# Butterflies and spectrum products of a long convolution moved from GpSimd to VectorE

## The chip, the cores and the metric

The kernel runs on one core of one Trainium2 chip. The metric is the device time of one execution in microseconds; several executions are taken, and their median counts. The core has TensorE (matmul, in the profile PE, its weight loads PEld), VectorE (DVE), ScalarE (ACT), GpSimd (POOL) and SyncE (SP, which issues the DMA transfers). Each engine takes its own instructions in order; semaphores hold an instruction until what it reads or overwrites is ready.

## What is computed

The reference is one layer of a hybrid backbone on 1024 latent tokens and 256 context tokens: a SwiGLU block, a mixer with four head groups, a second SwiGLU block, all in float32. The change lies in group B of the mixer, a Hyena long convolution of order 2 on 256 channels:

```
def long_conv(u, kf, bias):
    L = u.shape[1]
    U = jnp.fft.rfft(u, n=2 * L, axis=1)
    y = jnp.fft.irfft(U * kf[None], n=2 * L, axis=1)[:, :L]
    return y + u * bias

y = x1 * long_conv(v, kf[:, 0], bias[0])
y = x2 * long_conv(y, kf[:, 1], bias[1])
```

It is done once for the latents (L = 1024) and once for the context (L = 256). The other groups are windowed attention, dense attention and a gated linear attention (GLA).

## The kernel before

The kernel goes through the first SwiGLU block, the filters' spectra, the second half of that block, the projections with the mixer, the output projection and the second SwiGLU block. Matmuls of the big products are done three times per tile (L984 to L986): each operand is split into a high part, made on ScalarE (L56), and a low part, made on VectorE or GpSimd (L62).

A convolution splits time into 128 rows of J (8 for the latents, 2 for the context). The forward transform multiplies each of the J slices with a cosine and a sine matrix on TensorE (`forward_dft`, L217) and joins the J results by butterflies (`fft`, L120 to L168). Then comes the complex product with the filter's spectrum K (L365 to L370), a second `fft` into Z, which is the buffer of K, and the inverse matmuls (L380, L381), whose results are added to `u` times the bias and multiplied by the gate (L383, L385). For the latents this is done for two groups of 128 channels (`g`) and two orders (`o`), four passes one after another: each pass needs the result of the one before, or at least its buffers. For the context there are two passes of 256 channels, and J = 2 leaves `fft` after two operations of its first stage.

In `fft` the first stage gives sums `a` and differences `b`. The sums lead by `c` and `d` (L148, L149) to the rows with even number (L150 to L153), and this half ran on GpSimd; the differences lead to the odd rows (L158 to L166) on VectorE. Each operation is a separate instruction over all 128 partitions. The inverse matmuls take the rows in the order 0, 7, 6, 5, so they begin with an even one and go on with an odd one.

Around the convolution stand the projections (L984 to L986, evacuated by ScalarE at L1404, L1485 and L1491), the preparation of attention's queries and keys (`attn_prep`, L613 to L635: on ScalarE, VectorE and GpSimd), and, at higher priority, the context's convolution and its attention (L688 maxima, L702 their transposition, L762 and L763 scores, L740 values, L786 sums). A planner sets the order: it simulates the program's timeline with costs of its own and puts into each engine's queue what it thinks can run next. So an edit of one operation's engine changes the order of much around it, on all engines, until the output projection. `hyena_spectra` calls `fft` too, with buffers of its own, in the first SwiGLU block.

Of the kernel before, what the change touches and what calls it, by code (L numbers as in the profile page):

```python
# [12 lines left out]
ALU = mybir.AluOpType  # L13
# [102 lines left out]
def swp(a):  # L116
    return a[:, ::-1]


def fft(E, pool, J, W, stage1, dst, halves=None):  # L120

    nc = E.nc
    if J == 2:
        stage1(0, 1, ALU.add, dst[:, :, 0:1])
        stage1(0, 1, ALU.subtract, dst[:, :, 1:2])
        return
    if halves is None:  # L130
        a = pool.tile([128, 2, 4, W], F32, tag="fa", name="fa")
        b = pool.tile([128, 2, 4, W], F32, tag="fb", name="fb")
        for lo in (0, 2):
            stage1(lo, 2, ALU.add, a[:, :, lo:lo + 2])
        for lo in (0, 2):
            stage1(lo, 2, ALU.subtract, b[:, :, lo:lo + 2])
    else:
        a, b = halves

    def pair(f_re, f_im):  # L140
        step = f_im - f_re + J
        flat = dst.rearrange("p r j w -> p (r j) w")
        return flat[:, f_re:f_re + step + 1:step]

    g = nc.gpsimd
    c = pool.tile([128, 2, 2, W], F32, tag="fc", name="fc")
    d = pool.tile([128, 2, 2, W], F32, tag="fd", name="fd")
    g.tensor_tensor(out=c, in0=a[:, :, 0:2], in1=a[:, :, 2:4], op=ALU.add)  # L148
    g.tensor_tensor(out=d, in0=a[:, :, 0:2], in1=a[:, :, 2:4], op=ALU.subtract)  # L149
    g.tensor_tensor(out=pair(0, 0), in0=c[:, :, 0], in1=c[:, :, 1], op=ALU.add)  # L150
    g.tensor_tensor(out=pair(4, 4), in0=c[:, :, 0], in1=c[:, :, 1], op=ALU.subtract)
    g.tensor_tensor(out=pair(2, 6), in0=d[:, :, 0], in1=swp(d[:, :, 1]), op=ALU.add)
    g.tensor_tensor(out=pair(6, 2), in0=d[:, :, 0], in1=swp(d[:, :, 1]), op=ALU.subtract)  # L153

    v = nc.vector
    A, P = (pool.tile([128, 2, W], F32, tag=f"f{n}", name=f"f{n}") for n in "AP")
    B, M, e, f = (b[:, :, n] for n in (0, 1, 2, 3))
    v.tensor_tensor(out=A, in0=b[:, :, 0], in1=swp(b[:, :, 2]), op=ALU.add)  # L158
    v.tensor_tensor(out=B, in0=b[:, :, 0], in1=swp(b[:, :, 2]), op=ALU.subtract)
    v.tensor_tensor(out=P, in0=b[:, :, 1], in1=b[:, :, 3], op=ALU.add)  # L160
    v.tensor_tensor(out=M, in0=b[:, :, 1], in1=b[:, :, 3], op=ALU.subtract)
    v.tensor_tensor(out=e, in0=M, in1=swp(P), op=ALU.add)
    v.tensor_tensor(out=f, in0=swp(P), in1=M, op=ALU.subtract)
    for o, s, src, base in ((pair(1, 7), R_HALF, e, A), (pair(5, 3), -R_HALF, e, A),
                            (pair(3, 5), R_HALF, f, B), (pair(7, 1), -R_HALF, f, B)):
        v.scalar_tensor_tensor(out=o, in0=src, scalar=s, in1=base, op0=ALU.mult, op1=ALU.add)  # L166


def fft_from_dft(E, pool, J, W, banks, dst):

    nc = E.nc
    if J == 2:
        keep = pool.tile([128, 2, W], F32, tag="fk", name="fk")
        nc.scalar.activation(out=keep, in_=banks[1], func=ACTF.Copy)

        def stage1(lo, n, op, out):
            nc.vector.tensor_tensor(out=out.rearrange("p r j w -> p (r j) w"), in0=banks[0], in1=keep, op=op)
    else:
        keep = {}
        for q in (2, 3):  # L180
            k = pool.tile([128, 2, 2, W], F32, tag=("fc", "fd")[q - 2], name="fk")
            nc.scalar.activation(out=k, in_=banks[q], func=ACTF.Copy)
            keep[q] = k

        def stage1(lo, n, op, out):
            q = lo // 2
            nc.vector.tensor_tensor(out=out.rearrange("p r j w -> p j r w"), in0=banks[q], in1=keep[q + 2], op=op)
    fft(E, pool, J, W, stage1, dst)


def fft_from_sbuf(E, pool, J, W, src, dst):
    nc = E.nc

    def stage1(lo, n, op, out):
        h = J // 2
        nc.vector.tensor_tensor(out=out, in0=src[:, :, lo:lo + n], in1=src[:, :, lo + h:lo + h + n], op=op)
    fft(E, pool, J, W, stage1, dst)


def alloc_banks(E, J, W):  # L200
# [114 lines left out]
def hyena(E, P, seq, zrows, cw, cb, bias, dft, kspec, mixg, y_out):  # L315

    nc = E.nc
    J = 8 if seq == "lat" else 2
    T = 128 * J
    W = 128 if seq == "lat" else 256  # L320
    G = 256 // W
    pool = P["hy"]
# [31 lines left out]
    for g in range(G):  # L354
        u = token_major(0, g, "u")
        for o in range(2):
            X = pool.tile([128, 2, J, W], F32, tag="X", name="X")
            K = pool.tile([128, 2, J, W], F32, tag="K", name="K")
            E.load(K, kspec[o, g])
            forward_dft(E, pool, J, W, load_mats, u, X)  # L360
            b3 = bias[:, o, g * W:(g + 1) * W]
            nc.gpsimd.tensor_tensor(out=u, in0=u, in1=b3.unsqueeze(1).to_broadcast([128, J, W]), op=ALU.mult)
            t1 = pool.tile([128, J, W], F32, tag="fa", name="t1")
            t2 = pool.tile([128, J, W], F32, tag="fb", name="t2")
            nc.gpsimd.tensor_tensor(out=t1, in0=X[:, 0], in1=K[:, 0], op=ALU.mult)  # L365
            nc.vector.tensor_tensor(out=t2, in0=X[:, 0], in1=K[:, 1], op=ALU.mult)
            nc.vector.tensor_tensor(out=X[:, 0], in0=X[:, 1], in1=K[:, 1], op=ALU.mult)
            nc.vector.tensor_tensor(out=X[:, 1], in0=X[:, 1], in1=K[:, 0], op=ALU.mult)
            nc.gpsimd.tensor_tensor(out=X[:, 0], in0=t1, in1=X[:, 0], op=ALU.subtract)
            nc.vector.tensor_tensor(out=X[:, 1], in0=t2, in1=X[:, 1], op=ALU.add)  # L370
            gate = token_major(1 + o, g, "gate")
            Z = K
            fft_from_sbuf(E, pool, J, W, X, Z)
            jb = 512 // W
            for j0 in range(0, J, jb):
                ps = E.psum("s").rearrange("p (j w) -> p j w", j=jb)
                for j in range(jb):
                    f = (J - (j0 + j)) % J
                    m = load_mats(1, j0 + j)
                    nc.tensor.matmul(ps[:, j], lhsT=m[:, 0], rhs=Z[:, 0, f], start=True, stop=False)  # L380
                    nc.tensor.matmul(ps[:, j], lhsT=m[:, 1], rhs=Z[:, 1, f], start=False, stop=True)  # L381
                js = slice(j0, j0 + jb)
                nc.vector.tensor_tensor(out=u[:, js], in0=ps, in1=u[:, js], op=ALU.add)  # L383
                dst = u[:, js] if o == 0 else ytm[:, js, g * W:(g + 1) * W]
                nc.vector.tensor_tensor(out=dst, in0=u[:, js], in1=gate[:, js], op=ALU.mult)  # L385
            yield
# [1409 lines left out]
```

## Time and profile before

| | us |
|---|---|
| median of 3 runs | 2956.24 |
| the runs | 2952.4, 2956.24, 2982.59 |
| the profiled execution | 2959.08 |
| its span (first to last instruction) | 2957.3 |

| engine | busy us | share of the span |
|---|---|---|
| TensorE, matmul | 2749.6 | 93% |
| TensorE, weight load | 2180.1 | 74% |
| VectorE | 1898.0 | 64% |
| ScalarE | 1133.4 | 38% |
| GpSimd | 1118.4 | 38% |

The busy share is a mean over stages with different limits. A matmul's recorded length holds some overlap with its neighbour, so starts are the better measure of its pace. A group view gives for each kind of instruction how often and how long it ran and what ended the idle time in front of it; the order of time gives single instructions; the windows view gives a stretch's busy times with the granted TensorE clock, where 1.00 is 2.4 GHz and 0.50 is 1.2 GHz.

### The profile page before, as it was taken

How to read it: one execution, taken by the hardware profiler on the slowest of the kernel's cores; microseconds unless marked ns; L12 is line 12 of the kernel's file. 1: busy time of each engine (PE TensorE's matmuls, PEld its weight loads, DVE VectorE, ACT ScalarE, POOL GpSimd, SP SyncE). 2: the span in 40 equal slices, each digit the busy share in tenths (PEclk: the TensorE clock that was granted, in tenths of full speed). 3: DMA queues.
4: the chain of work that ended last, by engine and by line, in shares of the span. 5: the costliest groups of instructions: out<-in, count | busy, mean ns of one | idle time of the engine just before them, and what ended most of it. 6: DMA issues, size and time to landing. Idle time of an engine off the chain costs nothing.

```text
span 2957.3 us, 39868 instructions
## 1 busy us (share of the span) xinstructions
PE 2749.6 (93%) x14088; PEld 2180.1 (74%) x14088; DVE 1898.0 (64%) x3135; ACT 1133.4 (38%) x2051; POOL 1118.4 (38%) x980
## 2 busy tenths in 40 slices
PE   7899988899999888888988989989899999999998
PEld 5886776678788787776754544477898888878888
DVE  4978677754899955767657666662956555533447
ACT  5742222223333642224424434553743333333444
POOL 1334355544000214546415425463435555520002
PEclk9999999999999999899978979999999999999999
DMA  8654755342877563342462110264652222244445
GB/s 296 214 179 139 210 111 125 79 150 93 281 250 263 175 209 113 121 138 84 140 167 50 37 40 12 85 234 157 216 173 97 85 77 84 86 175 149 145 138 202
DMA packets 278460, 427.02 MB, mean 144 GB/s; under 512 B 97417, under 2 KB 163954, under 8 KB 276852
## 3 DMA queue, kind: packets, MB, share of 16 engines
q1 hardware_dynamic: 278260, 424.47, 44.6%
q8 instruction: 111, 1.82, 0.3%
q14 instruction: 89, 0.73, 0.1%
HBM read 345.14 MB, written 79.13 MB: 143 GB/s over the span
## 4 chain that ended last, share of the span: by engine, by line
PE 43%; DVE 5%; DMA 2%; issue 1%; ACT 1%; POOL 1%; SPq 0%; DVEq 0%; POOLq 0%; ACTq 0%
PE ps L986 11%; PE ps L984 10%; PE ps L985 10%; PE ps L740 2%; PE ps L762 1%; PE ps L688 1%; PE ps L763 1%; PE ps L550 1%; PE ps L535 1%; DVE wl L62 1%; DMA gd<-zf 1%; DVE mx L692 1%; PE ps L786 0%; PE ps L546 0%; PE ps L1139 0%
## 5 line engine op out<-in xcount | busy, mean ns | idle before, releaser
L56 ACT ACTIVATE wh<-raw 128x512 fp32r<-128x512 f32 x661 | 408.7, 625 | 513.6 <-PE ps L986 225.0
L62 POOL TENSOR_TENSOR wl<-raw,wh 128x512 fp32r<-128x512 f32 x221 | 328.1, 1489 | 558.1 <-ACT wh L56 342.1
L62 DVE TENSOR_TENSOR wl<-raw,wh 128x512 fp32r<-128x512 f32 x440 | 331.7, 760 | 170.9 <-ACT wh L56 113.2
L985 PE MATMUL ps<-gs,wh 128*128 128x512 f32 (+1 forms) x1056 | 376.5, 357 | 7.0 <-DVE gs L62 7.0
L986 PE MATMUL ps<-gs,wl 128*128 128x512 f32 (+1 forms) x1056 | 373.8, 356 | 2.9 <-DVE wl L62 2.9
L984 PE MATMUL ps<-gs,wh 128*128 128x512 f32 (+1 forms) x1056 | 351.8, 358 | 9.6 <-ACT gs L56 5.0
L984 PE MATMUL ps<-xh,wh 128*128 128x256 f32 (+2 forms) x952 | 320.8, 337 | 12.2 <-ACT zev L1404 5.6
L986 PE MATMUL ps<-xh,wl 128*128 128x256 f32 (+2 forms) x952 | 319.6, 337 | 10.9 <-POOL wl L62 6.4
L985 PE MATMUL ps<-xl,wh 128*128 128x256 f32 (+2 forms) x952 | 323.3, 340 | 0.0
L984 PE MATMUL ps<-t,wh 128*128 128x512 f32 x704 | 281.0, 399 | 11.0 <-DVE up L1077 6.2
L986 PE MATMUL ps<-t,wl 128*128 128x512 f32 x704 | 280.2, 399 | 1.9 <-DVE wl L62 1.9
L985 PE MATMUL ps<-t,wh 128*128 128x512 f32 x704 | 280.5, 398 | 0.0
L984 PE MATMUL ps<-b,wh 128*128 128x512 f32 x528 | 212.6, 403 | 20.6 <-DVE up L1074 19.7
L984 PEld LDWEIGHTS ps<-gs,wh 128*128 128x128 f32 x1056 | 200.3, 190 | 40.7 <-ACT gs L56 5.4
L985 PEld LDWEIGHTS ps<-gs,wh 128*128 128x128 f32 x1056 | 200.9, 190 | 35.9 <-DVE gs L62 7.7
L986 PEld LDWEIGHTS ps<-gs,wl 128*128 128x128 f32 x1056 | 200.5, 190 | 32.4 <-DVE wl L62 3.7
L56 ACT ACTIVATE wh<-s 128x512 fp32r<-128x512 f32 x176 | 110.4, 630 | 295.3 <-PE ps L985 152.1
L985 PE MATMUL ps<-b,wh 128*128 128x512 f32 x528 | 211.5, 401 | 0.0
L986 PE MATMUL ps<-b,wl 128*128 128x512 f32 x528 | 210.9, 399 | 0.2 <-POOL wl L62 0.2
L984 PEld LDWEIGHTS ps<-xh,wh 128*128 128x128 f32 (+1 forms) x952 | 182.3, 192 | 37.5 <-ACT zev L1404 7.2
L986 PEld LDWEIGHTS ps<-xh,wl 128*128 128x128 f32 (+1 forms) x952 | 181.8, 191 | 37.2 <-POOL wl L62 9.1
L919 POOL TENSOR_TENSOR tmp<-tmp 128x512 f32<-128x512 f32 (+1 forms) x18 | 24.7, 1374 | 482.1 <-ACT tmp L917 482.1
(369 smaller groups left out, 5906.5 us busy)
## 6 DMA issues: line engine op xcount, KB each, us to landing
raw<-in_w SPq DMA_DIRECT2D x308, 512.0 KB, 3.5
stg<-in_wmT SPq DMA_DIRECT2D x56, 512.0 KB, 4.1
hid<-g SPq DMA_DIRECT2D x88, 256.0 KB, 2.0
g<-hid SPq DMA_DIRECT2D x88, 256.0 KB, 2.7
m<-in_dft_lat SPq DMA_DIRECT2D x128, 128.0 KB, 2.7
raw<-in_wo SPq DMA_DIRECT2D x24, 512.0 KB, 3.8
x<-in_xT SPq DMA_DIRECT2D x36, 256.0 KB, 4.5
stg<-in_wmp SPq DMA_DIRECT2D x16, 512.0 KB, 10.6
```

What stands on the lines that cost most here:

```text
L56: nc.scalar.activation(out=hi, in_=src, func=ACTF.Copy)
L62: low = eng.tensor_tensor(out=lo, in0=src, in1=hi.bitcast(F32), op=ALU.subtract)
L535: nc.tensor.matmul(ps[:, t], lhsT=kt[32 * h:32 * h + 32, ts], rhs=qt[32 * h:32 * h + 32, ts], start=True, stop=True, tile_position=(32 * h ...
L550: nc.tensor.matmul(ps[:, i0:i0 + 64], lhsT=S[64 * p:64 * p + 64, c], rhs=qt[64 * p:64 * p + 64, 64 * c:64 * c + 64], start=False, stop=c % ...
L688: nc.tensor.matmul(ps, lhsT=qs, rhs=k1[:, lo:hi], start=True, stop=mo is None)
L692: nc.vector.tensor_reduce(out=mx[:, hh * nqt + t, bi:bi + 1], in_=ps, axis=AX.X, op=ALU.max)
L740: mm = nc.tensor.matmul(O[64 * hh:64 * hh + 64, s], lhsT=V[:, kt], rhs=p[hh], start=j == 0, stop=j == last)
L762: nc.tensor.matmul(ps, lhsT=k1[:, ks], rhs=q1[:, hh, a:b], start=True, stop=False)
L763: nc.tensor.matmul(ps, lhsT=k2[:, ks], rhs=q2[:, hh, a:b], start=False, stop=not banded)
L984: nc.tensor.matmul(ps, lhsT=wh(k), rhs=xh(k), start=start and k == 0, stop=False, skip_group_check=loose)
L985: nc.tensor.matmul(ps, lhsT=wh(k), rhs=xl(k), start=False, stop=False, skip_group_check=loose)
L986: nc.tensor.matmul(ps, lhsT=wl(k), rhs=xh(k), start=False, stop=stop and k == nk - 1, skip_group_check=loose)
```

## The change

`fft` gets a parameter `g`, the engine of the even half. The two callers in the convolution, `fft_from_dft` and `fft_from_sbuf`, pass VectorE; `hyena_spectra` passes nothing and stays on GpSimd. In the product, the first of the four multiplications (L365) and the subtraction (L369) go to VectorE as well.

```
-def fft(E, pool, J, W, stage1, dst, halves=None):
+def fft(E, pool, J, W, stage1, dst, halves=None, g=None):
...
-    g = nc.gpsimd
+    g = g or nc.gpsimd
     c = pool.tile([128, 2, 2, W], F32, tag="fc", name="fc")
     d = pool.tile([128, 2, 2, W], F32, tag="fd", name="fd")
     g.tensor_tensor(out=c, in0=a[:, :, 0:2], in1=a[:, :, 2:4], op=ALU.add)
...
-    fft(E, pool, J, W, stage1, dst)
+    fft(E, pool, J, W, stage1, dst, g=nc.vector)
...
-            nc.gpsimd.tensor_tensor(out=t1, in0=X[:, 0], in1=K[:, 0], op=ALU.mult)
+            nc.vector.tensor_tensor(out=t1, in0=X[:, 0], in1=K[:, 0], op=ALU.mult)
             nc.vector.tensor_tensor(out=t2, in0=X[:, 0], in1=K[:, 1], op=ALU.mult)
             nc.vector.tensor_tensor(out=X[:, 0], in0=X[:, 1], in1=K[:, 1], op=ALU.mult)
             nc.vector.tensor_tensor(out=X[:, 1], in0=X[:, 1], in1=K[:, 0], op=ALU.mult)
-            nc.gpsimd.tensor_tensor(out=X[:, 0], in0=t1, in1=X[:, 0], op=ALU.subtract)
+            nc.vector.tensor_tensor(out=X[:, 0], in0=t1, in1=X[:, 0], op=ALU.subtract)
```

On VectorE, in the second `fft` of the first pass (X is the product, K the tile of Z; rows before):

```order
L196 TENSOR_TENSOR fa<-X 128x2x256 x2
L196 TENSOR_TENSOR fb<-X 128x2x256 x2
L158 TENSOR_TENSOR fA<-fb 128x256
L160 TENSOR_TENSOR fP<-fb 128x256
L159 TENSOR_TENSOR fb<-fb 128x2x128
L161 TENSOR_TENSOR fb<-fb 128x2x128
```

and now:

```order
L196 TENSOR_TENSOR fa<-X 128x2x256 x2
L196 TENSOR_TENSOR fb<-X 128x2x256 x2
L148 TENSOR_TENSOR fc<-fa 128x512
L149 TENSOR_TENSOR fd<-fa 128x512
L158 TENSOR_TENSOR fA<-fb 128x256
L160 TENSOR_TENSOR fP<-fb 128x256
L150 TENSOR_TENSOR K<-fc 128x2x128
L151 TENSOR_TENSOR K<-fc 128x2x128
L152 TENSOR_TENSOR K<-fd 128x2x128
L153 TENSOR_TENSOR K<-fd 128x2x128
L159 TENSOR_TENSOR fb<-fb 128x2x128
L161 TENSOR_TENSOR fb<-fb 128x2x128
```

The even rows of K are now written ahead of four operations of the odd half, in one queue.

On GpSimd, in the first pass, from the bias product on (wl is a low part of a weight tile; rows before):

```order
L362 TENSOR_TENSOR tm<-tm,hy_bias 128x1024
L62 TENSOR_TENSOR wl<-raw,wh 128x512
L148 TENSOR_TENSOR fc<-fa 128x512
L149 TENSOR_TENSOR fd<-fa 128x512
L62 TENSOR_TENSOR wl<-raw,wh 128x512
L150 TENSOR_TENSOR X<-fc 128x2x128
L151 TENSOR_TENSOR X<-fc 128x2x128
```

and now, up to the bias product of the second pass:

```order
L362 TENSOR_TENSOR tm<-tm,hy_bias 128x1024
L62 TENSOR_TENSOR wl<-raw,wh 128x512 x2
L340 MEMSET raw 128x1
L342 MEMSET raw 128x1
L62 TENSOR_TENSOR wl<-raw,wh 128x512 x4
L627 TENSOR_TENSOR sw<-sw,sin 128x512 x2
L62 TENSOR_TENSOR wl<-raw,wh 128x512 x2
```

Low parts stand directly behind each other where butterflies stood between them.

On TensorE, where the last projection ends (k_13803 and q_13807 are the third pair of context heads, q_13723 and k_13719 the second, ytm the context's convolution result; rows before):

```order
L986 MATMUL ps<-wh,xl 128x256
L702 MATMUL ps<-ident,mm 4x128
L984 MATMUL ps<-wh,xh 128x256
L985 MATMUL ps<-wl,xh 128x256
L986 MATMUL ps<-wh,xl 128x256
L786 MATMUL ps<-acc,ones_87 64x256 x2
L801 MATMUL ps<-sq,ones_87 128x256
```

and now:

```order
L986 MATMUL ps<-wh,xl 128x256
L762 MATMUL ps<-q_13723,k_13719 128x256
L763 MATMUL ps<-q_13724,k_13720 128x256
L740 MATMUL ps<-p,V 64x256 x2
L688 MATMUL ps<-k_13803,q_13807 128x256
L402 MATMUL ps<-ident,ytm 128x128 x2
L762 MATMUL ps<-q_13807,k_13803 128x256
L402 MATMUL ps<-ident,ytm 128x128 x2
L740 MATMUL ps<-p,V 64x256 x2
L762 MATMUL ps<-q_13807,k_13803 128x256
L688 MATMUL ps<-k_13803,q_13807 128x256 x2
L702 MATMUL ps<-ident,mm 4x128
```

The L702 of the third pair stood one projection group's end before the last projection; now fifteen matmuls of the context stand between the last projection and it.

## Rows read from the trace of the kernel before

**Rows 1.** Windows: stretch, us, busy time (instructions) by engine, PEclk, DMA share, GB/s.

```profile
1140.00:1400.00 260.00, 219.69 (x1282) 190.58 (x1281) 189.25 (x209) 75.44 (x148) 146.68 (x108) 0.91 0.34 111
1400.00:1500.00 100.00, 95.79 (x594) 83.64 (x592) 58.71 (x102) 43.51 (x98) 40.98 (x43) 0.98 0.43 136
1500.00:1550.00 50.00, 35.56 (x114) 19.25 (x113) 29.53 (x66) 10.66 (x28) 7.66 (x15) 0.72 0.78 198
```

**Rows 2.** Waits of TensorE, 1140 to 1400: total us, times, longest.

```profile
PE ps L380 <- DVE K L166: 17.0, 4, 6.1
PE ps L380 <- POOL K L150: 13.4, 4, 6.8
PE ps L984 <- ACT sw L1491: 7.2, 1, 7.2
PE ps L984 <- ACT zev L1404: 2.1, 1, 2.1
```

**Rows 3.** Order of time on TensorE: start, length, instruction, idle before it.

```profile
1177.93 0.79 PE L380 MATMUL ps<-K,m 128*128 128x128 f32 x2 [4.27 <-POOL K L150]
...
1182.48 0.79 PE L380 MATMUL ps<-K,m 128*128 128x128 f32 x2 [3.33 <-DVE K L166]
...
1242.02 0.79 PE L380 MATMUL ps<-K,m 128*128 128x128 f32 x2 [6.75 <-POOL K L150]
...
1249.31 0.79 PE L380 MATMUL ps<-K,m 128*128 128x128 f32 x2 [5.01 <-DVE K L166]
...
1370.67 0.49 PE L380 MATMUL ps<-K,m 128*128 128x128 f32 x2 [1.49 <-POOL K L150]
...
1377.49 0.79 PE L380 MATMUL ps<-K,m 128*128 128x128 f32 x2 [6.11 <-DVE K L166]
```

**Rows 4.** Order of time on VectorE, starts of passes 1 and 2.

```profile
1145.93 0.69 DVE L187 TENSOR_TENSOR fa<-ps,fk 128x512 f32<-128x512 f32 x1 [8.77 <-ACT fk L182]
1146.54 0.68 DVE L187 TENSOR_TENSOR fb<-ps,fk 128x512 f32<-128x512 f32 x1
...
1208.70 0.69 DVE L187 TENSOR_TENSOR fa<-ps,fk 128x512 f32<-128x512 f32 x1 [1.15 <-ACT fk L182]
```

**Rows 5.** Order of time on GpSimd: a low part, and the first even rows of K.

```profile
1148.60 1.48 POOL L62 TENSOR_TENSOR wl<-raw,wh 128x512 fp32r<-128x512 f32 x1
...
1176.98 0.90 POOL L150 TENSOR_TENSOR K<-fc 128x256 f32<-128x256 f32 x1
...
1241.07 0.90 POOL L150 TENSOR_TENSOR K<-fc 128x256 f32<-128x256 f32 x1
```

**Rows 6.** Order of time on VectorE: operations with GpSimd at rest.

```profile
1160.90 1.22 DVE L366 TENSOR_TENSOR t<-X,K 128x1024 f32<-128x1024 f32 x1
...
1314.24 0.42 DVE L162 TENSOR_TENSOR fb<-fb,fP 128x256 f32<-128x256 f32 x1
1314.58 0.42 DVE L163 TENSOR_TENSOR fb<-fP,fb 128x256 f32<-128x256 f32 x1
```

**Rows 7.** Order of time on VectorE: operations with GpSimd at work.

```profile
1148.84 1.51 DVE L160 TENSOR_TENSOR fP<-fb 128x256 f32<-128x256 f32 x1
1150.28 1.52 DVE L159 TENSOR_TENSOR fb<-fb 128x256 f32<-128x256 f32 x1
```

**Rows 8.** Windows as in rows 1, each begun where TensorE resumes.

```profile
1182.40:1189.00 6.60, 6.52 (x33) 6.33 (x34) 1.41 (x3) 1.11 (x2) 0.57 (x1) 0.59 0.32 99
...
1249.30:1255.00 5.70, 5.69 (x35) 5.65 (x36) 4.58 (x6) 2.42 (x5) 2.10 (x2) 0.71 0.47 153
1297.20:1303.00 5.80, 5.80 (x36) 5.80 (x37) 5.77 (x4) 1.78 (x4) 5.77 (x3) 0.73 0.67 206
...
1377.40:1385.00 7.60, 7.51 (x40) 6.20 (x41) 4.69 (x8) 2.44 (x6) 2.30 (x2) 0.68 0.49 148
```

**Rows 9.** Order of time on TensorE: steps of the context attention before the last projection.

```profile
1479.67 0.28 PE L762 MATMUL ps<-q,k 128*128 128x256 f32 x1
...
1499.65 0.27 PE L702 MATMUL ps<-ident,mm 128*4 128x128 f32 x1
```

More of the change, by code (lines that the diff above doesn't have):

```diff
@@ L196, in stage1 @@
         nc.vector.tensor_tensor(out=out, in0=src[:, :, lo:lo + n], in1=src[:, :, lo + h:lo + h + n], op=op)
-    fft(E, pool, J, W, stage1, dst)
+    fft(E, pool, J, W, stage1, dst, g=nc.vector)
 def alloc_banks(E, J, W):
```

## The prediction

> **What bounds the kernel now.** The windows view comes first [rows 1]: one row for each stretch, with the busy time of each engine, the granted TensorE clock and the DMA share. From 1140 to 1400 us, where the long convolution of the latents runs among projections, TensorE is busy 219.69 of 260 us, so 40.3 us are idle, and the clock is 0.91 of full speed on average. From 1400 to 1500 it misses only 4.2 us. From 1500 to 1550, behind the last projection, it is busy 35.56 of 50 us at 0.72.
>
> The waits view of TensorE for 1140 to 1400 [rows 2] names the idle time: 17.0 and 13.4 us for the spectrum tile K, which the inverse transform's matmuls (L380) read, 7.2 us for a copy on ScalarE (sw, L1491), 2.1 us for zev. The first two belong to this change. The order of time shows them pass by pass (a pass is one channel group with one order, four in all) [rows 3]: pass 1 waits 4.27 us for the even rows of K, written by GpSimd, and 3.33 for the odd rows, written by VectorE; pass 2 waits 6.75 and 5.01; pass 4 1.49 and 6.11; 3.4 us are left for pass 3. So TensorE is the bound of the kernel, and in this stretch it waits for the chain that makes K, on VectorE and GpSimd together.
>
> Each wait costs twice, since TensorE comes out of it at the lower of its two clock levels. In the four stretches of [rows 8], which start where it resumes, it is busy 6.52 us at 0.59, 5.69 at 0.71, 5.80 at 0.73 and 7.51 at 0.68. Busy time times missing clock is 2.7 + 1.6 + 1.6 + 2.4 = 8.3 us lost beside the 40.3.
>
> **Why the chain is slow: the two engines don't run side by side.** Alone, VectorE starts a 128x256 operation 0.34 us behind the one before (1314.24 to 1314.58) and needs 1.22 us for 128x1024 [rows 6]; fed from PSUM, a 128x512 follows another by 0.61 (1145.93 to 1146.54) [rows 4], which I take for every 128x512. While GpSimd works through low parts and butterflies, the same 128x256 operations follow each other by 1.44 us (1148.84 to 1150.28) [rows 7], the pace of GpSimd's 1.48 us operation beside them [rows 5]. So inside the chain the two add up: a GpSimd 128x512 that stays costs 1.44 - 0.34 = 1.10 us more. The Trainium skill, "SBUF — State Buffer", section "SBUF: two separate sides", has this as an exclusive lock on a port pair, which a GpSimd operation, or a VectorE operation with two SBUF inputs, holds for its whole length. By that rule each would cost its 1.48 us, and the sums below would give chains some 2 us longer; the row shows less, and the row is used.
>
> **What the change moves.** In every pass 12 butterflies (4 of 128x512, 8 of 128x256) and 2 products of 128x1024 go from GpSimd to VectorE; two short products per context pass go too. GpSimd keeps the bias, the low parts of weights (L62) and the rotation (L627). No DMA is added or taken away.
>
> *Pass 1.* VectorE up to the first even rows of K: 16 operations of 128x512 at 0.61, 17 of 128x256 at 0.34 and 6 of 128x1024 at 1.22 are 9.8 + 5.8 + 7.3 = 22.9 us. Beside them the trace has four low parts (one of them in [rows 5]) in the stretch, 4.4 us; the bias product falls beside PSUM-fed operations, which keep their pace under it [rows 4], and is taken as free. From 1145.93 that is 27.3 us: 1173.2, where GpSimd now ends at 1176.98 + 0.90 = 1177.9 [rows 5]. TensorE arrives at 1177.93 - 4.27 = 1173.7 now [rows 3] and has five more projection matmuls ahead of it (138 become 143), about 1174.6: no wait. The odd rows need 11 more operations and one low part, 3.7 + 1.1, so 1178.0 against 1182.5. TensorE has four short matmuls and 17 projections in between, some 2.9 us, and waits 0.5 where it waited 3.33.
>
> *Pass 2.* From the third L187 at 1208.70 [rows 4]: again 16, 17 and 6, one short extra, 23.2 us, and six GpSimd operations and a piece of the bias product, 7.2: 1239.1 against 1242.0 [rows 5]. The wait of 6.75 becomes 3.6. The odd rows follow 7.8 us later, and 30 projection matmuls instead of 5 now stand in between, 6.8 us: the 5.01 goes to 0.1.
>
> *Passes 3 and 4, and the rest.* The gain of the even rows is 4.7 and 2.9, of the odd rows 4.5 and 2.4 (pass 2's odd rows: 1246.9 against 1249.3). Pass 3's 3.4 us go under with either. In pass 4 the 1.49 goes, and TensorE is at the odd rows that much earlier; 6.11 + 1.5 - 3.5 leaves 4. The wait for sw arises because ScalarE stands at a copy whose input is made by L628, which stands in VectorE's queue behind a product; in the new order that L628 follows the L187 directly. Its 7.2 us can go to 0 or stay; I take 1.5, nearer to nothing because of this place. zev keeps its 2. Left: 0.5 + 3.7 + 0 + 4 + 1.5 + 2 = 12 of 40.3 us, a gain of 28; of the clock's 8.3 the same share comes back, 6. Together **34 us**.
>
> The short context products save VectorE and GpSimd time under work that hides them (95.8 of 100 us are busy there [rows 1]) and count as nothing; without that cover they would bring 2 us.
>
> **What it costs.** Projections are also the cover of the context attention behind. The planner has put more of them ahead of the end of the latents' convolution: 153 are left behind it, where 244 of that kind were. When the last one is through, the new order still has the second half of one context head pair, two maxima and the transposes ahead of L702 of the third pair, which now stands before the last three projections. Now these steps run from 1479.67 to 1499.65 [rows 9], 20 us, among projections. Uncovered they are some 15 short TensorE groups with two hand-overs to VectorE; I estimate 8 us at the lower clock that this stretch has [rows 1]. Bounds are 4 us (TensorE's share alone) and 20 (no step gets shorter).
>
> The sum: 34 - 8 = 26 us less. The profiled run took 2959.1 us, so 2933; the median of the runs lies 2.8 us lower, so **2930 us**, 0.9% less. About 1% is what a measurement can tell from no change here, and it is reported so.
>
> A rule that speaks against the change: the Trainium skill, "VectorE: DVE Perf Modes", section "The TRN2 errata — SBUF-src ops pay a fixed extra latency per instruction", gives (N+151)/0.96 ns, an estimate of 0.42 us for each moved 128x256. The trace agrees with the length (0.42 [rows 6]), but the next one starts after 0.34; by the rule's length the moved butterflies would cost some 0.6 us more per pass, and nothing above changes by more than 3 us.
>
> **The rivals.** *The tail hides itself* (0.22): the loads of the latents' attention begin when the last projection ends, and the exposed steps run while they land; 34 and no loss gives 2922. For it speaks that the stretch behind is not full anyway [rows 1]; against it, that TensorE takes its queue in order. *The cover is what decides* (0.20): the low parts crowd into the chain, eight per pass for four to six, 3.3 us per pass or some 13 us with the clock's 3, and the tail keeps 16 of its 20 us: 34 - 16 - 16 = 2 us less, 2954. For it speaks that GpSimd, freed, reaches its low parts sooner: six L62 stand together in the new order. Against it: these wait for TensorE to free their buffers. *VectorE becomes the bound* (0.06): every VectorE operation keeps the contended pace. Then the 17 + 16 + 6 of a pass cost 1.10 more each, 43 us for the 4 to 7 us taken above; 36 us more per pass against a gain of 10 at most, far above 3000. It ends slower as soon as about 12 more GpSimd operations than counted stand beside each chain (13 us a pass, 52 in all, against 34 less 8, and the clock on top); the trace has four to eight there. *The forecast* has 0.52.
>
> **How the numbers follow.** The forecast's own range is 2915 to 2945 (sw at 0 or 7, the tail at 4 or 16). The best case, no wait left and no tail, is 2959 - 46 - 3 = 2910; the second rival reaches 2956. The range 2910 to 2956 leaves out the third rival and the outer ends, under 0.2. Faster by over 1% means under 2926.7: most of the first rival and a third of the forecast, 0.36. Slower by over 1%: 0.06. Within 1%: 0.58.
>
> **What would show it.** In the profile after: waits for K under 10 us in place of 30; 128x256 operations on VectorE at 0.4 us for the most part; the chains from L187 to the first K at about 27 and 30 us; the clock from 1140 to the end of the fourth pass near 0.97; and behind the last projection a longer stretch of half-busy TensorE. If the waits stay and VectorE's operations are still near 1.5 us, the price of shared time was wrong; if they go and the end doesn't come nearer, the tail was.

## The result and the profile after

The changed kernel takes 2917.65 us in the median of four runs (2914.08 to 2921.99) against 2959.23 for the kernel before; the ratio is 0.9863 with a 95% interval of 0.9835 to 0.9892, so 1.1 to 1.65% faster. The profiled execution has a span of 2915.7 us, 41.6 us less than before. The forecast was 2930 us with a range of 2910 to 2956; the time lies in it, on its fast side, and it is faster by over 1%, where the larger share of the chances stood on less than that. A second measurement, told further below, gave 2923.17 us and 0.6 to 1.4% faster.

The windows view of the kernel after has the columns and the first two stretches of [rows 1]:

```profile
1140.00:1400.00 260.00, 246.47 (x1475) 213.06 (x1474) 184.31 (x286) 90.30 (x179) 87.68 (x68) 0.99 0.42 134
1400.00:1500.00 100.00, 86.04 (x486) 68.37 (x485) 61.11 (x129) 33.41 (x81) 24.05 (x37) 0.85 0.58 159
```

From 1140 to 1400 us TensorE now lacks 13.5 us where it lacked 40.3, its clock is 0.99 instead of 0.91, and GpSimd is busy for 88 us instead of 147, while VectorE, which took over 14 operations per pass, is busy for 184 us, 5 fewer than before. The stretch of low clock has come forward with the end of the projections, into 1400 to 1500.

The waits of TensorE from 1140 to 1400 in the kernel after, as in [rows 2] (total us, times, longest):

```profile
PE ps L380 <- DVE K L166: 6.5, 2, 5.1
...
PE ps L380 <- issue: 1.5, 1, 1.5
PE ps L380 <- DMA m<-in_dft_lat: 1.4, 1, 1.4
PE ps L380 <- PE ps L986: 0.9, 1, 0.9
```

The 30.4 us for K have become 6.5 for odd rows and 1.5 for an even row of pass 4 (the row with "issue"). The last two rows are of pass 2. The 0.9 us belong to its even rows: TensorE resumes at 1231.72, 0.1 us behind their write, as it does in pass 4. The 1.4 us end at 1240.68, where a transfer of m and the last write of K's odd rows (1240.70) both come to their end. So 8.9 to 10.3 us are waits for K. The wait for sw is gone. The order of time on VectorE shows the chains, as in [rows 4, 5]: the first L187 of pass 1 and the third of pass 2, each with the first write of K's even rows, which has moved to this engine.

```profile
1148.66 0.69 DVE L187 TENSOR_TENSOR fa<-ps,fk 128x512 f32<-128x512 f32 x1 [8.77 <-ACT fk L182]
...
1175.66 0.41 DVE L150 TENSOR_TENSOR K<-fc 128x256 f32<-128x256 f32 x1
...
1204.77 0.69 DVE L187 TENSOR_TENSOR fa<-ps,fk 128x512 f32<-128x512 f32 x1 [0.44 <-ACT fk L182]
...
1231.21 0.41 DVE L150 TENSOR_TENSOR K<-fc 128x256 f32<-128x256 f32 x1
```

Pass 1 takes 27.4 us to the end of that write (32.0 before), pass 2 takes 26.9 (33.3).

Where the 41.6 us came from is best read between marks that belong to the program and not to the clock: the first L187, the last projection's matmul, the first L444 (the gated linear attention, which opens the latents' attention stage) and the first L1139 of the output projection. The windows view of TensorE alone has the columns stretch, us, busy (instructions), PEclk, DMA share, GB/s. The kernel before:

```profile
1145.93:1500.06 354.13, 309.61 (x1837) 0.93 0.37 117
1500.06:1547.80 47.74, 33.44 (x107) 0.71 0.82 207
1547.80:1972.40 424.60, 392.15 (x1840) 0.92 0.24 72
```

and the kernel after:

```profile
1148.66:1461.20 312.54, 297.83 (x1818) 0.98 0.41 130
1461.20:1512.78 51.58, 36.50 (x128) 0.70 0.82 209
1512.78:1933.10 420.32, 395.63 (x1847) 0.92 0.24 73
```

The convolution and the projections take 41.6 us less: idle time falls from 44.5 to 14.7 us, busy time by 11.8. Of the latter I put some 3 us down to the 21 matmuls that now stand behind the last projection (107 become 128) and the rest, about 9, to the clock, which rises from 0.93 to 0.98. The stretch behind the last projection is 3.8 us longer. So 37.8 us are won by the first L444; the attention stage gives 4.3 more, the rest of the program, ahead of and behind these marks, takes 0.4 back.

### The profile page after: what moved, and what is told of

Read it like the earlier page. It is cut to its first block, busy times and chain, and to the rows that moved or that the text cites. A ratio compares the mean times of both kernels' runs of the same rounds, so it can differ in the third digit from the quotient of the medians.

```text
span 2915.7 us, 39869 instructions
## 1 busy us (share of the span) xinstructions
PE 2743.1 (94%) x14088; PEld 2169.4 (74%) x14088; DVE 1876.8 (64%) x3195; ACT 1133.9 (39%) x2051; POOL 1035.0 (35%) x920
## 4 chain that ended last, share of the span: by engine, by line
PE 63%; DVE 9%; DMA 4%; issue 2%; POOL 1%; ACT 1%; SPq 1%; DVEq 0%; ACTq 0%; POOLq 0%
PE ps L984 17%; PE ps L985 17%; PE ps L986 17%; PE ps L740 2%; PE ps L762 1%; PE ps L688 1%; PE ps L763 1%; DVE wl L62 1%; PE ps L550 1%; DMA kslat<-ks 1%; PE ps L535 1%; SPq L50 1%; PE ps L217 1%; POOL wl L62 0%; PE ps L546 0%
## 5 line engine op out<-in xcount | busy, mean ns | idle before, releaser
L62 POOL TENSOR_TENSOR wl<-raw,wh 128x512 fp32r<-128x512 f32 x221 | 332.9, 1511 | 601.4 <-ACT wh L56 336.1
L62 DVE TENSOR_TENSOR wl<-raw,wh 128x512 fp32r<-128x512 f32 x440 | 331.8, 760 | 170.9 <-ACT wh L56 111.0
L984 PE MATMUL ps<-b,wh 128*128 128x512 f32 x528 | 213.0, 403 | 21.5 <-DVE up L1074 20.6
L62 DVE TENSOR_TENSOR wl<-s,wh 128x512 fp32r<-128x512 f32 x132 | 118.0, 894 | 125.9 <-ACT wh L56 79.5
```

What stands on the lines that cost most here:

```text
L62: low = eng.tensor_tensor(out=lo, in0=src, in1=hi.bitcast(F32), op=ALU.subtract)
L984: nc.tensor.matmul(ps, lhsT=wh(k), rhs=xh(k), start=start and k == 0, stop=False, skip_group_check=loose)
```

## Experiments

Theory A is the prediction's: VectorE and GpSimd take turns wherever both work on SBUF, a GpSimd operation beside the chain costs it about 1.1 us, and TensorE waits for the chain (on VectorE and GpSimd, from a pass's L187 to the first even rows of K). Against it stood theory B (no turns, an operation costs its own engine only), theory C (the gain comes from the planner's new order) and, from a row of the profile after, theory D (VectorE keeps its pace and GpSimd's operation is held). For the stretch behind the last projection theory T says that exposed steps run while the transfers land, against theory C there, the price that the prediction put on them.

### The butterflies alone

```
-            nc.vector.tensor_tensor(out=t1, in0=X[:, 0], in1=K[:, 0], op=ALU.mult)
+            nc.gpsimd.tensor_tensor(out=t1, in0=X[:, 0], in1=K[:, 0], op=ALU.mult)
...
-            nc.vector.tensor_tensor(out=X[:, 0], in0=t1, in1=X[:, 0], op=ALU.subtract)
+            nc.gpsimd.tensor_tensor(out=X[:, 0], in0=t1, in1=X[:, 0], op=ALU.subtract)
```

> The butterflies are on VectorE as in the change, the two products of L365 and L369 stay on GpSimd as before. Theory A (two engines with SBUF operands take turns, so that a GpSimd operation beside the chain costs VectorE its time): the even half still gains on VectorE (1.44 becomes 0.34 to 0.61 us for each pair that took turns); only the product's part of the chain stays at about 9.4 us (1160.90 to 1170.23 before) where 6.9 would do; the chain of pass 1 from the first L187 to the first even rows of K takes 29 to 30 us (32 before, 27.3 after), the waits for K are 15 to 20 us, the time 2930 to 2942. Theory B (no turns; an operation costs only its own engine): 12 butterflies more stand on VectorE in the chain, where GpSimd did them beside it; the chain is as long as before or longer, the waits for K are 30 us or more, the time 2955 or more. Theory C (the gain came from the planner's new order and not from the chains): any time, with chains as before.

Measured: 2914.73 us, ratio 0.987 (0.9835 to 0.9905). The waits of TensorE from 1140 to 1400:

```profile
PE ps L380 <- issue: 13.6, 4, 7.7
...
PE ps L380 <- DVE K L166: 2.4, 1, 2.4
```

and its windows between the marks:

```profile
1143.36:1468.94 325.58, 302.70 (x1834) 0.97 0.39 126
1468.94:1517.13 48.19, 30.76 (x115) 0.82 0.86 212
1517.13:1932.30 415.17, 388.15 (x1845) 0.92 0.24 75
```

The chain of pass 1 is 29.6 us long and the waits for K are 16.0, both as theory A has them; theory B's 30 us of waits are excluded. The time is not as theory A has it: from the first L187 to the first L444 this kernel wins 28.1 us, which would give 2925 from the 2953.08 that the kernel before took on the same chip (and 2931 from the 2959 on which theory A's numbers were made), and it is as fast as the whole change because in its profile the attention stage behind takes 9.4 us less than before. That stage is not touched by the edit; how much it differs between executions is told below.

### The products alone

```
-    fft(E, pool, J, W, stage1, dst, g=nc.vector)
+    fft(E, pool, J, W, stage1, dst)
...
-    fft(E, pool, J, W, stage1, dst, g=nc.vector)
+    fft(E, pool, J, W, stage1, dst)
```

> The two products are on VectorE as in the change, the even half of the butterflies stays on GpSimd as before. Theory A: the product's part of the chain falls from 9.4 to some 7 us, the rest keeps taking turns; chain of pass 1 about 29.5 us, waits for K 18 to 24 us, time 2938 to 2950. Theory B: the product alone carries the gain (3.3 and 3.4 us on GpSimd against 1.2 each on VectorE, less nothing for the butterflies): the chains are as short as with the whole change, the time 2915 to 2925. If the gains of this and of the butterflies alone add up to the whole change's 40 us, the parts are independent.

Measured: 2939.54 us, ratio 0.9955 (0.9932 to 0.9979). The waits:

```profile
PE ps L380 <- DVE K L166: 15.3, 4, 5.7
...
PE ps L380 <- POOL K L150: 6.2, 2, 4.4
```

and the window from the first L187 to the last projection:

```profile
1143.13:1493.03 349.90, 312.60 (x1843) 0.94 0.37 118
```

The chain of pass 1 is 29.7 us, the waits for K are 21.5 us and the time is 2939.5, all inside theory A's numbers. Each part alone shortens the chain of pass 1 by 2.3 us, both together by 4.5: in this pass the parts add up within 0.1 us. TensorE's gain to the first L444 does not: 28.1 us with the butterflies, 4.2 with the products, 37.8 with both. Nor do the medians: 38.4 and 13.5 us alone, 32 to 42 together. So the parts are not independent in time; why, no run shows.

### Eight more GpSimd operations beside each chain

```
+            extra = [nc.gpsimd.tensor_tensor(out=ytm[:, 0:4, g * W:(g + 1) * W], in0=u[:, 0:4], in1=u[:, 4:8], op=ALU.add) for _ in range(8 if J == 8 else 0)]
             gate = token_major(1 + o, g, "gate")
```

> The changed kernel with eight more GpSimd additions of 128x512 in each of the four passes, beside the chain; their output is overwritten later and nothing waits for it in the chain. Theory A: those beside SBUF-fed operations cost VectorE 1.1 us each, some six to eight a pass; the chain of pass 1 grows from 27.3 to 34 or 36 us, that of pass 2 from 26.8 to as much, the waits for K grow by 20 to 30 us, the time is 2940 to 2955. Theory B: the chains keep their length, the time is 2915 to 2922. Theory D (VectorE's queue wins, as in the stretch from 1229.39 us of the profile after, where one low part on GpSimd took 6.93 us while VectorE kept 0.34 us per operation): the chains grow by under 2 us, single GpSimd operations take several us, the time is 2917 to 2927.

Measured: 2961.19 us, ratio 1.0021 (0.9995 to 1.0046); the whole gain is gone. On TensorE the order of the first two passes is the changed kernel's. VectorE's order of time in pass 1, from the first L187 to the first even rows of K:

```profile
1143.81 0.69 DVE L187 TENSOR_TENSOR fa<-ps,fk 128x512 f32<-128x512 f32 x1 [8.77 <-ACT fk L182]
...
1179.40 0.42 DVE L150 TENSOR_TENSOR K<-fc 128x256 f32<-128x256 f32 x1
```

The chain is 36.0 us long where it was 27.4: 8.6 us for eight operations, 1.07 each. In pass 2 it is 37.4 instead of 26.9, or instead of 29.0 in the second profile of the changed kernel, which makes 1.05 each. The time lies above theory A's 2955: the waits for K grew to 19.5 us only, by 9 where 20 to 30 were expected, but those for copies on ScalarE (raw, zev) and for R come to 20.5 beside them. To the first L444 the kernel needs 403.6 us, as much as the kernel before (401.9), with all butterflies and products on VectorE. This is the plainest evidence for theory A: the moved work is done where the change puts it, the order on TensorE is the same, and only GpSimd's unrelated work beside it has grown. The chains carry that evidence better than the time, since the eight operations also stand ahead of low parts in GpSimd's queue. It also sets the price of the third rival: eight more operations per pass are enough to take the whole gain, not twelve. One thing is not separated: GpSimd is also slower operation for operation (0.90 us for a 128x256 in [rows 5], where VectorE starts one every 0.34), and where the even half alone decides when K is ready, the change gains by that as well.

### The price by itself

A kernel that computes nothing of the layer runs VectorE and GpSimd operations on tiles of their own, in parts that start together.

```
def dve(n, count):
    nc.vector.tensor_tensor(out=oD[:, :n], in0=a[:, :n], in1=b[:, :n], op=ALU.mult)   # count times
def pool(count):
    nc.gpsimd.tensor_tensor(out=oP, in0=c[:, :512], in1=d[:, :512], op=ALU.mult)      # count times
```

> Nothing of the layer is computed; the kernel runs stretches of VectorE and GpSimd operations on tiles of their own, alone and beside each other. Alone: VectorE 0.34 us for each 128x256, GpSimd 1.25 to 1.30 for each 128x512. Theory A: beside each other a VectorE operation with two SBUF inputs starts every 1.44 us (128x256), 1.7 (128x512) or 2.2 to 2.3 (128x1024), GpSimd at the same pace; one with a PSUM input keeps 0.61. Theory B: both keep their own pace. Theory D: VectorE keeps its pace and GpSimd's operations are stretched to the end of VectorE's queue; in the last three stretches, where one GpSimd operation becomes ready in the middle of VectorE's row of 128x256, it takes 5 to 10 us and VectorE stays at 0.34, while theory A has it take 1.5 us and cost VectorE one gap of 1.1.

The order of time, with equal operations grouped (start, length of the whole row, count). GpSimd alone and beside 128x256, 128x512, 128x1024, 128x512 from PSUM and a one-input 128x512 on VectorE:

```profile
19.98 10.64 POOL L880 TENSOR_TENSOR oP<-c,d 128x512 f32<-128x512 f32 x8 [19.54 <-ACT c L864]
31.34 16.75 POOL L880 TENSOR_TENSOR oP<-c,d 128x512 f32<-128x512 f32 x12 [0.72 <-ACT c L864]
65.19 19.95 POOL L880 TENSOR_TENSOR oP<-c,d 128x512 f32<-128x512 f32 x12 [17.10 <-ACT c L864]
98.75 26.34 POOL L880 TENSOR_TENSOR oP<-c,d 128x512 f32<-128x512 f32 x12 [13.62 <-ACT c L864]
130.67 16.07 POOL L880 TENSOR_TENSOR oP<-c,d 128x512 f32<-128x512 f32 x12 [5.58 <-ACT c L864]
152.90 16.74 POOL L880 TENSOR_TENSOR oP<-c,d 128x512 f32<-128x512 f32 x12 [6.17 <-ACT c L864]
```

Alone a GpSimd 128x512 takes 1.33 us. Beside two-input SBUF operations a pair takes 1.40, 1.66 and 2.20 us (16.75, 19.95 and 26.34 over 12). Beside PSUM-fed operations GpSimd keeps 1.34 us, which supports the bias product counted as free. Beside the one-input operation the pair takes 1.40 us, so that form takes turns as well, which no row of the kernel before had shown.

In this kernel every VectorE operation writes what the one before it wrote and waits for it; alone they follow each other by 0.46 us (24 in 11.00) and not by 0.34. In its last three parts, where one GpSimd operation becomes ready in the middle of a row, that operation takes 1.31 to 1.38 us and not theory D's 5 to 10. A second kernel has them write two tiles in turn, and lets GpSimd's operations become ready behind the first operation of a row:

```
def row(n, count):
    nc.vector.tensor_tensor(out=o2[r % 2][:, :n], in0=a[:, :n], in1=b[:, :n], op=ALU.mult)   # r counts
def part(n, count, pools):
    nc.vector.tensor_tensor(out=oD[:, :n], in0=a[:, :n], in1=b[:, :n], op=ALU.mult)
    nc.gpsimd.tensor_tensor(out=oP, in0=oD[:, :512], in1=d[:, :512], op=ALU.mult)            # pools times
    row(n, count)
```

> Nothing of the layer is computed. VectorE runs rows of operations that write two outputs in turn, so that each overlaps with the one before it (0.34 us for each 128x256); GpSimd's 128x512 becomes ready behind the first of a row. Theory A (strict turns): a single GpSimd operation takes about 1.4 us, a row of 40 grows by 1 us from 13.6; six of them cost 6 us. Theory D (GpSimd comes in only where VectorE's row pauses; seen in two low parts of 6.3 and 6.9 us beside gapless rows): the single operation lasts to the end of the row, some 13 us for 40 of 128x256, 18 for 30 of 128x512, 19 for 16 of 128x1024, and the rows keep their pace; of six, the first lasts as long and the others follow behind the row at 1.3 each.

VectorE's order of time: 30 operations alone, 40 with one GpSimd operation, 40 with six.

```profile
10.17 10.09 DVE L869 TENSOR_TENSOR o<-a,b 128x256 f32<-128x256 f32 x30
...
21.54 14.57 DVE L869 TENSOR_TENSOR o<-a,b 128x256 f32<-128x256 f32 x40
...
52.06 19.89 DVE L869 TENSOR_TENSOR o<-a,b 128x256 f32<-128x256 f32 x40
```

GpSimd's: the one and the six.

```profile
21.70 1.38 POOL L875 TENSOR_TENSOR oP<-oD,d 128x512 f32<-128x512 f32 x1 [21.26 <-DVE oD L873]
...
52.22 8.38 POOL L875 TENSOR_TENSOR oP<-oD,d 128x512 f32<-128x512 f32 x6 [13.88 <-DVE oD L873]
```

Forty operations at 0.336 us are 13.45; with one GpSimd operation they take 1.1 us more, with six 6.4, so 1.07 each. Theory A holds to the tenth, theory D doesn't show here.

### More and fewer of the context's steps behind the last projection

Two kernels put the last projections ahead of the context's attention in the program and give the attention a priority of 0 or of 800 rows:

```
+    proj_fm(15)
+    proj_tm(1)
+    with tc.high_priority(offset=0):     # the other kernel: offset=800
-    with tc.high_priority(offset=LEAD):
         run_attention(EC, attn_pools(cts, "c", **R_), "ctx")
-    proj_fm(15)
-    proj_tm(1)
```

> The changed kernel with the last projections (15 and the second of tokens by columns) ahead of the context's attention in priority: from the projections' end on, nearly all of that attention stands uncovered, four head pairs where the changed kernel has half of the second and the third. Theory T (the stretch behind the last projection is a fixed 48 us or so, set by the transfers that begin there; exposed steps run inside it): the last projection ends some 10 us sooner, the stretch to the first L444 grows by no more than that, to 50 to 62 us, the time is 2908 to 2928. Theory C (each exposed head pair costs what the prediction took, 8 us for the steps of one): two to three more pairs exposed, 16 to 24 us more, the time 2930 to 2942.

> The same two lines exchanged, but the attention's priority raised so far that its third pair is through its transposition (L702) 57 rows of TensorE ahead of the last projection, as in the kernel before. Theory T: the stretch from the last projection to the first L444 is 48 us again (51.6 in the changed kernel), the last projection ends 2 to 3 us later, the time is that of the changed kernel, 2914 to 2920. Theory C: the 8 us come back, the time is 2907 to 2911.

Measured: 2936.26 us with nearly all of that attention exposed, 2921.04 with its third pair covered, beside 2923.17 for the changed kernel on the same chip. TensorE's windows from the first L187 to the last projection and from there to the first L444, with offset 0:

```profile
1140.29:1451.05 310.76, 295.56 (x1791) 0.98 0.39 129
1451.05:1531.41 80.36, 61.95 (x216) 0.72 0.56 140
```

and with offset 800:

```profile
1150.25:1469.86 319.61, 304.10 (x1844) 0.98 0.40 130
1469.86:1513.71 43.85, 33.65 (x103) 0.65 0.92 225
```

With the third pair covered the projections end 7 us later and the stretch behind is 7.7 us shorter: 363.5 us together, as in the changed kernel (364.1). So what the change exposes costs nothing that these profiles can tell, and theory C's 2907 to 2911 us did not come; the 2921 are at the end of theory T's 2914 to 2920. With four pairs exposed it is the other way round: the stretch grows to 80.4 us, where theory T allowed 62, the kernel loses 27 us to the first L444, some 9 to 14 for each of the two to three pairs more, and the 2936 us lie in theory C's range. So theory T holds for the steps that the change exposes and fails for more of them; for those, a price of 8 us for a pair is of the right size. Where between the two the cover ends was not tested.

### The low parts on VectorE as well, and without the change

All projections but those of the first two calls (0, 2 and 4) get their low parts (L62) on VectorE, first in the changed kernel, then in the kernel before:

```
-def proj_fm(*ts):
+def proj_fm(*ts, lo="dve"):
...
-    w = {t: load_w(P, i["wig"] if t == 16 else i["wi"][t], 8, m) for t in ts}
+    w = {t: load_w(P, i["wig"] if t == 16 else i["wi"][t], 8, m, (lo, lo)) for t in ts}
...
-    proj_fm(0, 2)
-    proj_fm(4)
+    proj_fm(0, 2, lo="pool")
+    proj_fm(4, lo="pool")
...
-    w = load_w(P, i["wi"][(8 if kind == "a" else 11) + row])
+    w = load_w(P, i["wi"][(8 if kind == "a" else 11) + row], 8, 128, ("dve", "dve"))
```

(and the same pair of engines in `proj_tm`).

> The changed kernel with the low parts of all projections from the third on (L62) on VectorE too, so that GpSimd has only bias and rotation beside the chains. Theory A (turns): a low part beside the chain costs VectorE about 1.0 us when GpSimd does it (0.93 to 1.1 measured) and 0.67 when VectorE does it itself; four to six per pass, so the chains of 27.4 and 26.8 us become 1 to 3 us shorter, the waits for K fall from 8 to under 6 us, the time is 2908 to 2918. Theory B (no turns): each low part lengthens the chain by its 0.67 us, 3 to 4 us a pass, the waits for K grow to 15 us or more, the time is 2925 to 2935.

> The kernel before, even half and products on GpSimd, with only the low parts of the projections (L62, from the third projection on) moved to VectorE. Theory A: the chain keeps taking turns between butterflies on both engines; a low part costs it 0.67 where it cost 1.0 to 1.1, so the chain of pass 1 is 30 to 32 us (32 before), waits for K 24 to 30 us, the stretch from the first L187 to the first L444 392 to 402 us (402 before), the time 2945 to 2955. Theory L (the low parts by themselves bring the 15 us that they brought on top of the change, since projections get their weights sooner, whatever the chains do): that stretch takes 385 to 389 us, the time is 2935 to 2942.

Measured: 2883.63 us on top of the change, ratio 0.9775 (0.974 to 0.9811), the fastest kernel of this study; 2935.72 us without it, ratio 0.9939 (0.9919 to 0.996). TensorE's windows from the first L187 to the last projection and on to the first L444, with the change:

```profile
1143.84:1438.97 295.13, 289.76 (x1802) 1.00 0.42 137
1438.97:1492.73 53.76, 42.87 (x171) 0.84 0.83 202
```

and without it:

```profile
1145.02:1495.10 350.08, 311.79 (x1843) 0.95 0.36 118
1495.10:1538.48 43.38, 31.07 (x103) 0.72 0.92 227
```

On top of the change the waits for K are all but gone (0.9 us from 1140 to 1400), TensorE runs at full clock to the last projection, and the first L444 comes 15 us sooner than in the changed kernel (348.9 against 364.1). Theory B, by which the chains would have grown, falls. But my size was wrong: 2908 to 2918 was expected. The chain of pass 1 is 2.0 us shorter, as worked out; that of pass 2 is 29.6 us, longer than in the changed kernel, and TensorE still doesn't wait, because more projections stand between its arrival and K. That points to theory L for a part of the gain: low parts that don't queue on GpSimd let projections go ahead. Without the change the outcome is mixed. The chain of pass 1 (30.0 us) and the stretch to the first L444 (393.5 us, 8.4 less than before) are theory A's; the waits for K, 22 us, are under its 24 to 30; and the median is theory L's, since 16 us are won in all, half of them outside that stretch. To the first L444 the two edits together win more than the sum of each alone (53.0 us against 37.8 and 8.4). Some 12 us more of the difference lie in the attention stage (408.3 us against 420.3).

### The same kernel again

> The changed kernel as it is, for a second profile of it beside the others and for the spread of its times. From the first transform of the latents to the last projection 321 us as in its first profile, from there to the first L444 51.6, from L444 to the output projection (L1139) 420. If the last stretch comes out other than 420 by more than 3 us, the differences of 415 to 432 us that the kernels show there are spread between executions; if it comes out at 420 again, they belong to the order that the planner made.

Measured: 2923.17 us in the median of nine runs (2907.47 to 2947.3), ratio 0.9903 (0.9864 to 0.9942); the profiled execution took 2935.98. (The first profile had 312.5 us to the last projection, not the 321 of the expectation.) TensorE's windows between the same marks as above, and then 40 us of the attention stage:

```profile
1141.03:1452.56 311.53, 297.81 (x1817) 0.98 0.40 130
1452.56:1504.08 51.52, 36.61 (x128) 0.70 0.81 209
1504.08:1951.70 447.62, 422.95 (x1847) 0.86 0.22 70
...
1824.10:1864.10 40.00, 40.00 (x122) 0.50 0.01 1
```

The same 40 us, 320 us behind the first L444, in the first profile:

```profile
1832.80:1872.80 40.00, 38.66 (x165) 1.00 0.15 44
```

Up to the first L444 the two executions agree within about 1 us (363.1 and 364.1), although pass 2 differs. On VectorE, its third L187 and the first even rows of K:

```profile
1197.12 0.69 DVE L187 TENSOR_TENSOR fa<-ps,fk 128x512 f32<-128x512 f32 x1 [0.43 <-ACT fk L182]
...
1225.71 0.41 DVE L150 TENSOR_TENSOR K<-fc 128x256 f32<-128x256 f32 x1
```

That chain takes 29.0 us here and 26.9 in the first profile; the two kernels with the last projections put first have 29.0 as well. TensorE waits 10.9 us for K from 1140 to 1400. Behind the first L444 the two executions run alike for 280 us (the L702 of the last pair follows the first L444 by 284 us in both), and there they part: in the first TensorE is at full clock, in the second it works through 40 us at 0.50, the lower of its two levels (1.2 GHz), busy all the time, and that stage is 27 us longer, all of it busy time for the same 1847 matmuls (422.95 against 395.63 us). In the 40 us ahead of these it was busy for 38.3 us in both, at 0.83 and 0.64. The same program with the same order does both. So the 2 to 16 us by which the attention stages of the other kernels of this study differ from that of the kernel before can't be put down to their edits from single profiles, while the stretch up to the first L444 can be compared to about 1 us.

## Why the prediction was right, and where not

**Turns between the engines: right.** The price of 1.10 us for a GpSimd operation beside the chain was taken from [rows 6, 7]; by itself it measured 1.07, and 1.05 to 1.07 in the kernel with eight more. The Trainium skill, "SBUF — State Buffer", section "SBUF: two separate sides", has the loser blocked for the whole instruction; GpSimd's 1.33 us would then be the price, and the runs show about 0.26 us less.

**Lengths of the chains: right for pass 1, and for pass 2 by the second execution.** 27.3 us were worked out for pass 1 and 27.4 measured, with 1.36 us of wait at its odd rows instead of 0.5. For pass 2 the sum gave 30.4: the first profile has 26.9, the second 29.0 with a wait of 3.01 us (3.6 forecast). In the second, five GpSimd operations take turns in the chain where the sum had six; the first profile differs by a low part that did not, below.

**Waits and clock: right, the clock term a little small.** 28 us of idle time were to go from 1140 to 1400 and 26.8 went (40.3 to 13.5). The odd rows of pass 4 kept 5.1 us where 4 were left in the sum; the wait for sw went altogether where 1.5 were kept. For the clock 6 us were taken, and about 9 came back; the four stretches of [rows 8] had not held all of the loss. That is some 36 us where the sum had 34, and 3 more idle us were won between 1400 and the last projection, which the sum did not look at. Most signs came as named: 0.41 us for most 128x256, chains of 27 and 27 to 29 us, a clock of 0.98 to the last projection. Under 10 us of waits for K was missed by a little: 8.9 to 10.3 in the first profile and 10.9 in the second.

**The tail: wrong.** The step that failed is "I estimate 8 us", with 4 us as its lower bound. I took the exposed steps as time to add. The covered variant shows that they cost nothing here: 363.5 against 364.1 us to the first L444. The price is of the right size for pairs exposed beyond these; what failed is that it was charged to steps that the stretch had room for. The stretch is 3.8 us longer, but the projections end sooner by the 3 us or so of the matmuls that moved behind them. This is the first rival, "the tail hides itself", which had a chance of 0.22 and a time of 2922 us. What I used against it, that TensorE takes its queue in order, does not decide it: TensorE's two longest waits there end with transfers, which SyncE issues in order. The order of time of the kernel after, on TensorE:

```profile
1466.47 0.27 PE L702 MATMUL ps<-ident,mm 128*4 128x128 f32 x1 [1.44 <-DVE mm L696]
...
1471.96 0.77 PE L763 MATMUL ps<-q,k 66*128 66x256 f32 x2 [3.64 <-DMA q<-mh]
...
1499.59 0.80 PE L763 MATMUL ps<-q,k 66*128 66x256 f32 x2 [3.88 <-DMA q<-ml]
```

and on SyncE:

```profile
1488.74 6.66 SPq L50 DMA_DIRECT2D S<-in_s  x4
...
1496.43 0.64 SPq L50 DMA_DIRECT2D q<-mh  x1
```

The exposed L702 and the wait behind it are over at 1472; the next wait of over 1 us ends at 1499.6 with a transfer of q that SyncE could issue only at 1496 to 1498, behind others that had kept its queue. The DMA share of the whole stretch is 0.82, before as after. That the transfers are what gives the exposed steps their room is argued from these rows and not shown by a run of its own.

**The other rivals.** *The cover decides* did not happen: the low parts beside the chain of pass 1 were four, as counted, and the tail kept nothing. *VectorE becomes the bound* did not happen either, but the kernel with eight more GpSimd operations shows its mechanism at work, and nearer than I put it: eight operations more per pass took 39.5 us to the first L444 (403.6 against 364.1). By the prediction's own price six per pass, 26 us, would have eaten the forecast gain; its twelve does not follow from its terms.

**The sum.** 34 us less 8 were forecast; 38 less nothing were measured up to the first L444, and the rest of the profiled execution added 4, within what two executions of this program differ by. With the tail at nothing the forecast's own terms give 2959 - 34 - 3 = 2922, 4 us from the median. The narrower range of 2915 to 2945 was not worked out right at its lower end: sw at 0 and the tail at 4 give some 2924, so with these bounds the measured 2918 falls out of it, and only the wider range, which allows for no tail, holds it by its terms.

## What to carry to other kernels

When VectorE and GpSimd both read SBUF beside each other, count their operations as one queue: moving work from GpSimd to VectorE can shorten the chain although VectorE has more to do, and what is left on GpSimd beside it still costs about 1.1 us per 128x512. Operations fed from PSUM did not take part in the turns here. Before a price is put on steps that lose their cover, look at what the stretch waits for anyway, transfers included, and let only the part that ends later than these count; here the steps of the change fitted in, and two to three pairs more did not. Compare kernels between marks of the program that lie before a stage whose clock differs between executions, and profile the same kernel twice before a few us are explained.

## What was not expected

At some places the turns were not kept, and not in every execution. The low part on GpSimd in pass 2, in the first profile:

```profile
1229.39 6.93 POOL L62 TENSOR_TENSOR wl<-raw,wh 128x512 fp32r<-128x512 f32 x1 [3.54 <-PE ps L985]
```

what VectorE did beside it there:

```profile
1229.93 0.41 DVE L158 TENSOR_TENSOR fA<-fb 128x256 f32<-128x256 f32 x1
```

and the same low part in the second profile of the same program:

```profile
1221.75 1.76 POOL L62 TENSOR_TENSOR wl<-raw,wh 128x512 fp32r<-128x512 f32 x1 [3.54 <-PE ps L985]
```

In the first VectorE went on at 0.34 us per 128x256 and GpSimd's operation lasted 6.93 us, until VectorE paused; in the second they took turns, it lasted 1.76, the rotation behind it came into the chain too, and the chain was 2.1 us longer, two turns. Three other profiles have one such low part each in pass 2, a few operations further on: 6.33 us with the butterflies alone, 6.32 with eight more GpSimd operations, 6.27 with four pairs exposed, each beside a row of VectorE without a gap. The two kernels that were made to show it (GpSimd's operation becoming ready in a gapless row) had 1.31 to 1.38 us beside 128x256 each time, so what decides it stays open. And the attention stage, with the clock at 0.50 for 40 us of unbroken work in one execution and at 1.00 there in another, differs by 27 us, two thirds of what the change brought.
